# First layer's FFN input projection as seven block products with block sums, and the residual parked in DRAM

## The chip, the cores and the metric

The kernel runs on one core of a Trainium2 chip. The metric is the device time of one execution in microseconds (us). Before the change the median of three runs is 2299.05 us (2296.88 to 2300.37). The engines are named as the profile names them: PE (TensorE matmul), PEld (its weight loads), DVE (VectorE), ACT (ScalarE), POOL (GpSimd), SP (SyncE, which here issues every DMA).

## What is computed

A trunk of two layers over 512 latent tokens and 256 context tokens, 1024 channels. Each layer has a token-mixing block and a SwiGLU FFN with 2816 hidden channels. Only the FFN matters here:

```python
def swiglu(h, w_in, w_out):
    gate, up = jnp.split(h @ w_in, 2, axis=-1)
    return (jax.nn.silu(gate) * up) @ w_out

x = x + g2 * swiglu(modulate(rmsnorm(x, norm2_g[l]), sh2, sc2), w_ffn_in[l], w_ffn_out[l])
```

In the first layer it runs over all 768 tokens, in the second over the 512 latent ones. All data are float32.

## The kernel before

Activations lie with channels on the partitions and tokens along the free axis. A product of float32 data is made as three fp32r matmuls: each operand is split into a rounded part (`hh`, `whi`, written by a cast on ACT) and the rest (`hl`, `wlo`, a subtraction on DVE), and `group_steps` (L193) adds `whi·hh`, `whi·hl` and `wlo·hh` up in one PSUM bank for each of the 128-channel blocks k of the contraction.

The first layer's FFN follows the output projection `wo` (`load_o`, `mul_o`, `done_o`, L1313 to L1327), whose `done_o` leaves the residual in the eight tiles `XT[f]`. `norm_seg` (L285) makes from them the eight tiles each of `hh` and `hl`, the FFN's input (768 tokens wide). Then the 22 hidden tiles of 128 channels are gone through in three chunks, `HID_CHUNKS` (L32). For a hidden tile i, `gate_f` (L1368) and `up_f` (L1376) each load a 128x1024 weight tile, split it, and multiply 8 blocks by 3 matmuls over 512 and over 256 tokens; ACT makes the silu of the gate, DVE multiplies by the up part, ACT and DVE split the result into `hidh` and `hidl`. At a chunk's end the output projection `fo` (`load_f`, `mul_f`, `done_f`, L1387 to L1407) multiplies the chunk's hidden tiles by their rows of `w_ffn_out`, for each of eight output blocks f, and `done_f` adds gate times product to `XT[f]` on DVE. The last chunk goes through `skewed_out` (L342): the latents of the last `SKEW` blocks first, then their context columns, under which the second layer's first norm is made.

Beside this DVE works off a list `bg` of background steps: `mods_rest` (L211) makes the modulation vectors as dot products, one 128x1024 multiply-and-accumulate (L225) for each piece. `bg_step` (L544) puts n of them behind a given DVE instruction; in the FFN it is called after each hidden tile and in each `load_f`, with the rest of the list shared out by `slots`. Where `tc.manual_schedule(engines={PE})` holds, PE's order is that of the program text; elsewhere, and on the other engines, a scheduler lists instructions by program order as they come ready. Every engine then runs its list in order, and so does SP with the DMAs.

SBUF is shared out in tags: 31 `unit` tiles of 128x768 (`hh`, `hl`, `XT`, temporaries), 6 `wide` ones, 3 `whi` and 3 `wlo` of 128x1024, 2 raw weight tiles, 14 `hid` tiles. PSUM has 8 banks: `mm` 3, `s` 2, `t` 2, `o` 1.

## Time and profile before

| | |
|---|---|
| median of 3 runs | 2299.05 us |
| the profiled execution | 2298.55 us, its span 2296.8 us |
| PE busy | 2251.3 us, 98% of the span |
| DVE, ACT, POOL busy | 1447.4, 853.4, 291.0 us |
| mean granted clock of TensorE | 0.993 of full speed |
| DMA | 281 MB, mean 122 GB/s |

A matmul's record in the trace covers its way through the array and overlaps with the next one, so what a matmul costs is read from the distance between starts, not from its duration. The first layer's FFN lies at about 800 to 1355 us: chunk 1 up to 936, its output projection to 1004, then two chunks of seven tiles with theirs.

### The profile page before, as it was taken

To read this page: it belongs to the slowest core of one execution; us is meant where nothing else is said; L and a number is where in the kernel's file an instruction comes from. 1 tells how busy PE (TensorE), PEld (TensorE's weight loads), DVE (VectorE), ACT (ScalarE), POOL (GpSimd) and SP (SyncE) were. 2 spreads that over 40 slices of the span, in tenths; PEclk is the share of its full clock that TensorE was granted. 3 is DMA by queue.
4 is the path that set the end of the run, shared out by engine and by line. 5 is a ranking of instruction groups with operands and counts; after the bars stand their busy time and mean duration, and the time that the engine had idled before them with its cause. 6 is when DMAs were issued, how large, how long until landed. Compare 5 with 4: busy or idle time off the path is not lost.

```text
span 2296.8 us, 33406 instructions
## 1 busy us (share of the span) xinstructions
PE 2251.3 (98%) x12896; PEld 1954.3 (85%) x12896; DVE 1447.4 (63%) x2629; ACT 853.4 (37%) x1612; POOL 291.0 (13%) x294
## 2 busy tenths in 40 slices
PE   8999999999999999999999999999999999999998
PEld 4989899999878888888888888888888778888887
DVE  6887878887776455735522358878877655433334
ACT  5335444445512242112112244555445424222223
POOL 0112211112133010000000021311111221000000
PEclk9999999999999999999999999999999999999999
DMA  7432324444454324524521224233444443423322
GB/s 288 135 101 74 106 95 125 138 125 138 136 201 168 94 92 136 156 89 151 187 70 65 71 95 129 87 118 109 123 124 123 169 165 100 150 93 97 97 95 80
DMA packets 100287, 281.07 MB, mean 122 GB/s; under 512 B 12048, under 2 KB 21408, under 8 KB 100128
## 3 DMA queue, kind: packets, MB, share of 16 engines
q1 hardware_dynamic: 100128, 278.93, 38.0%
q8 instruction: 102, 1.67, 0.3%
q14 instruction: 57, 0.47, 0.1%
HBM read 228.15 MB, written 24.52 MB: 110 GB/s over the span
## 4 chain that ended last, share of the span: by engine, by line
PE 66%; DVE 2%; issue 1%; ACT 1%; DMA 0%; POOL 0%; POOLq 0%; SPq 0%; DVEq 0%; ACTq 0%
PE fg L199 13%; PE fu L199 13%; PE fo L199 13%; PE gt L199 6%; PE wo L199 5%; PE br L199 4%; PE gq L605 2%; PE o L1082 2%; PE s L1005 2%; PE nv L199 1%; PE nk L199 1%; PE pt L1057 1%; PE nq L199 1%; PE ga L199 1%; PE va L199 1%
## 5 line engine op out<-in xcount | busy, mean ns | idle before, releaser
L181 ACT CAST whi<-wraw 128x1024 fp32r<-128x1024 f32 (+1 forms) x274 | 285.2, 1041 | 624.3 <-PE fo L199 181.7
L182 DVE TENSOR_TENSOR wlo<-wraw,whi 128x1024 fp32r<-128x1024 f32 (+1 forms) x274 | 338.6, 1236 | 211.1 <-ACT whi L181 206.2
L1039 POOL TENSOR_SCALAR pt<-pt,sm 128x768 f32<-128x768 f32 (+1 forms) x160 | 147.0, 919 | 760.6 <-DVE sm L1038 513.8
L787 DVE SCALAR_TENSOR_TENSOR y<-u,vec,y 128x783 f32<-128x783 f32 (+1 forms) x240 | 218.4, 910 | 1.5
L199 PE MATMUL gt<-hh,whi 128*128 128x512 f32 (+1 forms) x576 | 212.8, 369 | 0.0
L199 PE MATMUL gt<-hh,wlo 128*128 128x512 f32 (+1 forms) x576 | 205.4, 357 | 0.0
L199 PE MATMUL gt<-hl,whi 128*128 128x512 f32 (+1 forms) x576 | 205.2, 356 | 0.0
L199 PE MATMUL fo<-hidh,whi 128*128 128x512 f32 (+1 forms) x549 | 192.3, 350 | 0.0
L199 PE MATMUL fo<-hidh,wlo 128*128 128x512 f32 (+1 forms) x549 | 191.7, 349 | 0.0
L199 PE MATMUL fg<-hl,whi 128*128 128x512 f32 (+1 forms) x544 | 190.5, 350 | 1.1 <-POOL hl L305 0.8
L199 PE MATMUL fo<-hidl,whi 128*128 128x512 f32 (+1 forms) x549 | 191.5, 349 | 0.0
L199 PE MATMUL fg<-hh,whi 128*128 128x512 f32 (+1 forms) x544 | 190.4, 350 | 1.1 <-ACT hh L300 1.1
L199 PE MATMUL fg<-hh,wlo 128*128 128x512 f32 (+1 forms) x544 | 189.8, 349 | 0.0
L199 PE MATMUL fu<-hh,whi 128*128 128x512 f32 (+1 forms) x536 | 188.5, 352 | 0.6 <-ACT whi L181 0.6
L199 PE MATMUL fu<-hh,wlo 128*128 128x512 f32 (+1 forms) x536 | 188.3, 352 | 0.8 <-DVE wlo L182 0.8
L199 PE MATMUL fu<-hl,whi 128*128 128x512 f32 (+1 forms) x536 | 188.4, 352 | 0.0
L1059 ACT CAST pTh<-pt 128x384 fp32r<-128x384 f32 (+2 forms) x224 | 104.8, 497 | 138.4 <-PE pt L1057 137.6
L1060 DVE TENSOR_TENSOR pTl<-pt,pTh 128x384 fp32r<-128x384 f32 (+2 forms) x224 | 124.0, 569 | 20.2 <-ACT pTh L1059 19.1
L1400 DVE SCALAR_TENSOR_TENSOR xn<-fo,mods,xn 128x512 f32<-128x512 f32 (+1 forms) x75 | 48.3, 644 | 132.7 <-PE fo L199 132.7
L1383 DVE TENSOR_TENSOR sg<-fu,sg 128x512 f32<-128x512 f32 (+1 forms) x67 | 39.9, 596 | 138.3 <-PE fu L199 138.3
L199 PEld LDWEIGHTS gt<-hh,wlo 128*128 128x128 f32 x576 | 109.2, 190 | 16.2
L199 PEld LDWEIGHTS gt<-hh,whi 128*128 128x128 f32 x576 | 109.4, 190 | 11.1 <-ACT gtan L980 0.3
(269 smaller groups left out, 5419.0 us busy)
## 6 DMA issues: line engine op xcount, KB each, us to landing
wraw<-w_in SPq DMA_DIRECT2D x88, 512.0 KB, 3.5
wraw<-w_fi SPq DMA_DIRECT2D x88, 512.0 KB, 3.3
mraw<-wmod_t SPq DMA_DIRECT2D x80, 512.0 KB, 4.2
wraw<-w_fo SPq DMA_DIRECT2D x32, 448.0 KB, 3.3
gd<-gtan SPq DMA_DIRECT2D x48, 256.0 KB, 2.0
wraw<-w_br SPq DMA_DIRECT2D x24, 512.0 KB, 3.4
tg<-gd SPq DMA_DIRECT2D x24, 384.0 KB, 5.1
sraw<-wmod_s SPq DMA_DIRECT2D x16, 512.0 KB, 8.9
```

The lines of the kernel that those rows point to most:

```text
L181: act.copy(hi[:, :n], raw[:, :n])
L182: last_lo[0] = dve.tensor_sub(lo[:, :n], raw[:, :n], f32(hi[:, :n])).ins
L199: pe.matmul(ps[:, :c1 - c0], w[:, k, :], a[k][:, c0:c1], start=i == 0, stop=i == 3 * n - 1)
L605: pe.matmul(ps[:, :256], a[k][:, t * P:(t + 1) * P], w[:, o:o + 256], start=i == 0, stop=i == 3 * KT - 1)
L787: dve.scalar_tensor_tensor(y[:, :YW], u[:, t:t + YW], w, y[:, :YW], ALU.mult, ALU.add)
L1005: pe.matmul(o, Q[:, qc], k, start=i == 0, stop=i == 1)
L1039: pool.tensor_scalar(pt[:, :w], pt[:, :w], sm[:, 3:4], 1.0, ALU.mult, ALU.mult)
L1059: act.copy(hv[:, qi, k0:k0 + step, :], pv)
L1060: dve.tensor_tensor(lw[:, qi, k0:k0 + step, :], pv, f32(hv[:, qi, k0:k0 + step, :]), ALU.subtract)
L1082: pe.matmul(ops[:, o:o + n], v.rearrange("p z d -> p (z d)"), m, start=i == 0, stop=i == len(seq) - 1)
L1383: dve.tensor_mul(sg[:, c0:c1], ps[:, :c1 - c0], sg[:, c0:c1])
L1400: dve.scalar_tensor_tensor(XT[f][:, c0:c1], mrg["pf", f, c0][:, :c1 - c0], mods[l][:, 40 + f, v:v + 1], XT[f][:, c0:c1], ALU.mult, ALU.add)
```

## The change

It touches the first layer's FFN (and a little of what is just ahead of it); the second layer's keeps its form.

- From hidden tile 3 on, gate and up of a tile are made together as a 2x2 block product: the block rows are gate and up (A1., A2.), the block columns of A the first and second four of the eight k blocks, and B is the input cut at the same k and at token 384. Seven block products replace eight (Winograd's form of Strassen's scheme), each of 4 blocks by 3 matmuls over 384 tokens. Sums of weight blocks S1 to S4 are made on POOL, sums of input blocks T1 to T4 once ahead on DVE (`sums_of`, 16 background steps), and split into two fp32r parts each. Weight operands of 128x512 are split one by one (`parts`), two to a `whi`/`wlo` tile. Bank `a` collects A11·B11, S2·T2, S3·T3 and A22·T4 in turn, with copies (`snap`, ACT) of the sums between; bank `b` S1·T1 and S4·B22; bank `c` A12·B21. PE's order is written out by hand: `sw_mid(i)`, `sw_head(i+1)`, `sw_tail(i)`, `sw_head2(i+1)`.
- The chunks of the first layer become six: 3, 4, 4, 4, 3 and 4 hidden tiles (tag `hid` has 2 tiles there instead of 14, the others come from `wide`); the output projection thus runs six times over the eight blocks f, with fewer k each.
- The residual no longer stays in SBUF: `done_o` stores it to `xm` in DRAM, `load_f` reads it back for each f of each chunk, and after `done_f` it is stored again (but for the last chunk).
- The last two blocks of layer 0's modulation (18 background steps) move from the FFN into the `wo` stage, three in each `load_o`.
- The last chunk's `skewed_out` takes a skew of 6 instead of 3.

The core of the diff:

```diff
-HID_CHUNKS = ((0, 8), (8, 7), (15, 7))
+HID_CHUNKS = (((0, 3), (3, 4), (7, 4), (11, 4), (15, 3), (18, 4)), ((0, 8), (8, 7), (15, 7)))
+HALF = 384
@@ ahead of and in the wo stage
             bg_all()
+            if l == 0:
+                for blk in (10, 11):
+                    bg += mods_rest(0, blk)
             def load_o(f):
-                return load_wk(w_out[l, f], KT)
+                wk = load_wk(w_out[l, f], KT)
+                bg_step(3)
+                return wk
@@ done_o
                 square_acc(XT[f], AC, f, c0, c1)
+                if not last:
+                    dma.dma_start(xm[f, :, c0:c1], XT[f][:, c0:c1])
@@ FFN
-            slots = [6 if last else 3 * (NHID - 7) + 8 * 2]
+            chunks = HID_CHUNKS[l]
+            slots = [6 if last else (NHID - 3) + 8 * 5]
+            def sums_of(k):
+                def whole(i):
+                    q[i] = unit("tw")
+                    dve.tensor_add(q[i], f32(hh[k + i]), f32(hl[k + i]))
+                def t12():
+                    t = q["t"] = unit("ts")
+                    a, b = q[0], q[4]
+                    dve.tensor_sub(t[:, 0:HALF], a[:, HALF:TOK], a[:, 0:HALF])
+                    dve.tensor_sub(t[:, HALF:TOK], b[:, HALF:TOK], t[:, 0:HALF])
+                ...
+                def part(n):
+                    ...
+                    act.copy(h, t)
+                    dve.tensor_sub(lo, t, f32(h))
+                return [lambda: whole(0), lambda: whole(4), t12_part, t34_part]
+            def parts(src):
+                if cur[1] % 2 == 0:
+                    cur[0] = [mp.tile([P, 1024], F32R, tag=t, bufs=3, name=t) for t in ("whi", "wlo")]
+                ...
+                act.copy(hi, src)
+                last_lo[0] = dve.tensor_sub(lo, src, f32(hi)).ins
+            def sw_load(i):
+                g, u = [fp_.tile([P, 1024], F32, tag="sr", bufs=2, name="sraw") for _ in range(2)]
+                dma.dma_start(g, w_fi[l, i, 0])
+                dma.dma_start(u, w_fi[l, i, 1])
+            def sw_sum(d, name, a, b, op):
+                t = d[name] = fp_.tile([P, 512], F32, tag="S", bufs=4, name="ssum")
+                pool.tensor_tensor(t, d[a], d[b], op)
+            def sw_mul(d, bank, w, b, first):
+                ...
+                for k in range(4):
+                    for x, y in ((wh, bh), (wh, bl), (wl, bh)):
+                        pe.matmul(d[bank][:, :HALF], x[:, k, :], y[k], start=first and n == 0, stop=n == 11,
+                                  skip_group_check=True)
+            def sw_head(i):
+                sw_load(i)
+                sw_sum(d, "S1", "A21", "A22", ALU.add)
+                sw_sum(d, "S2", "S1", "A11", ALU.subtract)
+                sw_sum(d, "S3", "A11", "A21", ALU.subtract)
+                sw_mul(d, "a", "A11", "B11", True)
+                snap(d, "s1")
+            def sw_head2(i):
+                sw_mul(d, "b", "S1", "T1", True)
+            def sw_mid(i):
+                sw_mul(d, "a", "S2", "T2", False)
+                snap(d, "u2")
+                sw_sum(d, "S4", "A12", "S2", ALU.subtract)
+                sw_mul(d, "c", "A12", "B21", True)
+                dve.tensor_add(sg[:, 0:HALF], d["c"][:, :HALF], d["s1"])
+                act.activation(sg[:, 0:HALF], sg[:, 0:HALF], AF.Silu)
+                sw_mul(d, "a", "S3", "T3", False)
+                snap(d, "u3")
+                dve.tensor_add(d["u3"], d["b"][:, :HALF], d["u3"])
+            def sw_tail(i):
+                sw_mul(d, "a", "A22", "T4", False)
+                dve.tensor_mul(sg[:, 0:HALF], d["a"][:, :HALF], sg[:, 0:HALF])
+                sw_mul(d, "b", "S4", "B22", False)
+                dve.tensor_add(sg[:, HALF:TOK], d["b"][:, :HALF], d["u2"])
+                act.activation(sg[:, HALF:TOK], sg[:, HALF:TOK], AF.Silu)
+                dve.tensor_mul(sg[:, HALF:TOK], sg[:, HALF:TOK], d["u3"])
+                act.copy(q["h"], sg)
+                q["done"] = dve.tensor_sub(q["lo"], sg, f32(q["h"])).ins
             def load_f(f):
-                wk = load_wk(w_fo[l, f, :, k0:k0 + nk, :], nk)
+                if not last:
+                    XT[f] = unit("xt")
+                    dma.dma_start(XT[f], xm[f])
+                src = w_fo[l, f, :, k0:k0 + nk, :]
+                wk = load_wk(src, nk) if last or not lastc else parts(raw_w(src, nk * P)[:, :nk * P])
@@ chunk loop
+                    if not last:
+                        bg[:0] = [x for k in range(4) for x in sums_of(k)]
+                if ci and not last:
+                    while len(T) < 8:
+                        bg_step(1)
+                    manual = tc.manual_schedule(engines={PE})
+                    manual.__enter__()
+                    if ci == 1:
+                        sw_head(k0)
+                        sw_head2(k0)
+                    for i in range(k0, k0 + nk):
+                        sw_mid(i)
+                        if i + 1 < NHID:
+                            sw_head(i + 1)
+                        sw_tail(i)
+                        if i + 1 < NHID:
+                            sw_head2(i + 1)
+                        bg_step(-(-len(bg) // max(1, slots[0])), hid[i]["done"])
+                        slots[0] -= 1
+                    manual.__exit__(None, None, None)
...
-                        bg_step(-(-3 * len(bg) // max(1, slots[0])), hid[i]["done"])
-                    slots[0] -= 3
+                        bg_step(4 if not last else -(-3 * len(bg) // max(1, slots[0])), hid[i]["done"])
...
                             drain(mul_f(f, wk, (c0, c1, v)))
                             done_f(f, (c0, c1, v))
+                        if not last:
+                            dma.dma_start(xm[f], XT[f])
...
-                skewed_out(segs, TQ, load_f, mul_f, done_f, norms, SEG0_AT[2 * l + 1], SEG0_EVERY[2 * l + 1])
+                skewed_out(segs, TQ, load_f, mul_f, done_f, norms, SEG0_AT[2 * l + 1], SEG0_EVERY[2 * l + 1],
+                           SKEW if last else 6)
```

## Rows read from the trace of the kernel before

**Rows 1.** The page's first part: busy us, share of the span, instructions.
```profile
PE 2251.3 (98%) x12896; PEld 1954.3 (85%) x12896; DVE 1447.4 (63%) x2629; ACT 853.4 (37%) x1612; POOL 291.0 (13%) x294
```

**Rows 2.** Windows: stretch, length, busy us (instructions) of PE, PEld, DVE, ACT, POOL; PEclk, DMA share, GB/s.
```profile
836.70:853.40 16.70, 16.70 (x99) 14.78 (x98) 11.24 (x18) 4.54 (x7) 0.00 (x0) 1.00 0.47 158
936.00:1003.00 67.00, 67.00 (x384) 58.58 (x383) 41.83 (x66) 8.74 (x9) 0.00 (x0) 1.00 0.45 142
729.20:799.50 70.30, 69.42 (x395) 60.24 (x394) 30.15 (x42) 18.52 (x27) 3.93 (x4) 1.00 0.32 100
```

**Rows 3.** Waits of PE, 799 to 1360 us, longest entry: us in total, times, longest.
```profile
PE fg L199 <- POOL hl L305: 0.8, 1, 0.8
```

**Rows 4.** Timeline of PE, hidden tiles 1 to 3: start us, duration us, instruction.
```profile
834.16 0.28 PE L199 MATMUL fu<-hh,whi 128*128 128x256 f32 x1
834.28 0.28 PE L199 MATMUL fu<-hl,whi 128*128 128x256 f32 x1
...
836.68 0.40 PE L199 MATMUL fg<-hh,whi 128*128 128x512 f32 x1
...
853.36 0.40 PE L199 MATMUL fg<-hh,whi 128*128 128x512 f32 x1
```

**Rows 5.** Timeline of DVE, first output projection: the drains of two blocks f.
```profile
992.93 0.75 DVE L1400 SCALAR_TENSOR_TENSOR xn<-fo,mods,xn 128x512 f32<-128x512 f32 x1 [3.38 <-PE fo L199]
...
1001.33 0.75 DVE L1400 SCALAR_TENSOR_TENSOR xn<-fo,mods,xn 128x512 f32<-128x512 f32 x1 [3.38 <-PE fo L199]
```

**Rows 6.** Groups by shape, 700 to 1300 us: busy us, mean ns | idle before.
```profile
L225 DVE SCALAR_TENSOR_TENSOR mraw<-mraw,cb 128x1024 f32<-128x1024 f32 x50 | 60.7, 1223 | 22.6 <-DMA mraw<-wmod_t 22.1
...
L1383 DVE TENSOR_TENSOR sg<-fu,sg 128x512 f32<-128x512 f32 x22 | 15.2, 692 | 60.9 <-PE fu L199 60.8
L1384 ACT CAST hidh<-sg 128x512 fp32r<-128x512 f32 x22 | 13.7, 621 | 101.6 <-DVE sg L1383 101.6
...
L1400 DVE SCALAR_TENSOR_TENSOR xn<-fo,mods,xn 128x512 f32<-128x512 f32 x16 | 12.0, 750 | 22.1 <-PE fo L199 22.1
...
L1383 DVE TENSOR_TENSOR sg<-fu,sg 128x256 f32<-128x256 f32 x22 | 9.3, 424 | 16.0 <-PE fu L199 16.0
...
L305 POOL TENSOR_TENSOR hl<-nt,hh 128x512 fp32r<-128x512 f32 x6 | 7.8, 1314 | 9.1 <-ACT hh L304 9.1
...
L1400 DVE SCALAR_TENSOR_TENSOR xn<-fo,mods,xn 128x256 f32<-128x256 f32 x16 | 7.7, 483 | 19.9 <-PE fo L199 19.9
...
L1301 DVE SCALAR_TENSOR_TENSOR yl<-ys,yh 128x768 fp32r<-128x768 f32 x3 | 2.9, 954 | 4.0 <-ACT yh L1300 4.0
```

**Rows 7.** Timeline of POOL and DVE side by side, 639 and 674 us (branch projection).
```profile
639.00 2.00 POOL L590 TENSOR_TENSOR ys<-ys,tg 128x512 f32<-128x512 f32 x2 [17.53 <-DVE tg L589]
639.64 0.42 DVE L589 SCALAR_TENSOR_TENSOR tg<-tg,br 128x256 f32<-128x256 f32 x1 [0.72 <-PE br L199]
...
674.54 2.97 POOL L590 TENSOR_TENSOR ys<-ys,tg 128x512 f32<-128x512 f32 x2 [2.60 <-issue]
674.65 2.26 DVE L225 SCALAR_TENSOR_TENSOR mraw<-mraw,cb 128x1024 f32<-128x1024 f32 x1
676.85 0.08 DVE L225 DVE_READ_ACCUMULATOR mraw<-mraw,cb 128x1 f32 x1
```

**Rows 8.** Timeline of DVE: the end of hidden tile 1.
```profile
839.69 0.42 DVE L1385 TENSOR_TENSOR hidl<-sg,hidh 128x256 fp32r<-128x256 f32 x1
```

**Rows 9.** The page's DMA issues: line, engine, count, KB each, us to landing.
```profile
wraw<-w_fi SPq DMA_DIRECT2D x88, 512.0 KB, 3.3
```

**Rows 10.** Windows of a DMA peak, and of PE idling and its clock (columns of rows 2).
```profile
654.00:656.00 2.00, 1.38 (x8) 0.88 (x7) 2.00 (x5) 0.00 (x0) 0.00 (x0) 1.00 1.01 391
658.00:660.00 2.00, 2.00 (x11) 1.67 (x10) 2.00 (x5) 0.26 (x1) 1.22 (x1) 1.00 1.04 414
...
1361.00:1362.00 1.00, 0.35 (x2) 0.14 (x2) 1.00 (x2) 0.40 (x1) 1.00 (x1) 1.00 0.86 291
1363.00:1366.00 3.00, 3.00 (x14) 2.72 (x14) 1.57 (x3) 1.53 (x3) 1.32 (x2) 0.50 0.28 112
```

More of the change, by code (lines that the diff above doesn't have):

```diff
@@ L162, in trunk @@
     xd = dp.tile([KT, P, TOK], F32, name="xd")
+    xm = dp.tile([KT, P, TOK], F32, name="xm")
     gd = [dp.tile([24, P, TOK], F32, name="gd%d" % l) for l in range(DEPTH)]
@@ L340, in begin, with skewed_out @@
         pump(1)
-    def skewed_out(segs, T, load, mul, done, norms, at, every):
+    def skewed_out(segs, T, load, mul, done, norms, at, every, skew=SKEW):
         s0, s1 = segs
         whole = segs if s0[2] != s1[2] else [(0, T, 0)]
-        n0 = KT - SKEW
+        n0 = KT - skew
         wks = {}
@@ L1362, in hidden @@
                     hid[i] = dict(sg=fp_.tile([P, TOK], F32, tag="sg", bufs=2, name="sg"),
[L1363 to L1365 removed]
+                                  h=fp_.tile([P, TOK], F32R, tag="hid", bufs=HB, name="hidh") if last or i % 4 == 0
+                                  else wide("hidh", F32R)[:, :TOK],
+                                  lo=fp_.tile([P, TOK], F32R, tag="hid", bufs=HB, name="hidl")
+                                  if i % (2 if last else 4) == 0 else wide("hidl", F32R)[:, :TOK])
                 return hid[i]
+            HB = 14 if last else 2
             def gate_f(i, c0, c1, tag=None):
@@ new lines, in sw_mul @@
+            def sw_mul(d, bank, w, b, first):
+                if first:
+                    d[bank] = psum(dict(a="mm", b="s", c="t")[bank], "sw")
+                wh, wl = parts(d[w])
+                bh, bl = side(b)
+                n = 0
+                for k in range(4):
+                    for x, y in ((wh, bh), (wh, bl), (wl, bh)):
+                        pe.matmul(d[bank][:, :HALF], x[:, k, :], y[k], start=first and n == 0, stop=n == 11,
+                                  skip_group_check=True)
+                        n += 1
@@ L1394, in mul_f, with psum_out @@
                 c0, c1, _ = seg
-                ps = mrg["pf", f, c0] = psum_any("fo")
+                ps = mrg["pf", f, c0] = psum_any("fo") if last or lastc else psum_out()
                 yield from group_steps(ps, wk, gh, gl, c0, c1)
+            def psum_out():
+                turn[0] += 1
+                return psum(("mm", "t", "s", "mm", "t")[turn[0] % 5], "fo")
             def done_f(f, seg):
@@ L1422, in trunk @@
                         drain(up_f(1, c0, c1))
-                for i in range(k0, k0 + nk):
+                    if not last:
[18 more added lines that the diff above has]
+                    manual.__exit__(None, None, None)
+                for i in () if ci and not last else range(k0, k0 + nk):
                     if i >= 2:
```

61 lines of the change are left out of this document (54 added, 7 removed).

## The prediction

> **What bounds the kernel now.** I read the engines' busy shares first: PE is busy 98% of the span [rows 1]. Then the windows by stage: in a hidden tile of the first layer's FFN and in its output projection PE is busy for the whole stretch, DVE for 11.24 of 16.70 us at most, ACT for 4.54, POOL not at all [rows 2]. Then PE's waits: over the whole FFN the longest entry is 0.8 us in total [rows 3]. So this stage is a dense row of matmuls, and what a matmul less saves is its distance to the next start. The same rows show what may not grow: DVE has the least room.
>
> **PE, what is removed.** Tile 2 begins at 836.68, tile 3 at 853.36 [rows 4]: 16.68 us for 48 matmuls over 512 tokens and 48 over 256, so one pair costs 0.3475 us; the 256 ones are 0.12 apart [rows 4]. A matmul over 384 tokens is not in the trace; it lies halfway between the two, so I take half a pair, 0.1738 us. A new tile has 7 x 4 x 3 = 84 of them: 14.59 us, each block product 2.085 us. That is 2.09 us less for each of 19 tiles: **39.6 us**, just the eighth of the work. The output projections keep their matmuls (22 x 8 x 3 pairs) and only change their order: 8.40 us for a block f with eight k [rows 5], so 1.05 for each k. PE's floor is therefore 2298.55 - 39.6 = 2259 us; all else can only add to that, but for the handover at the end.
>
> **DVE, POOL and ACT in a new tile.** Prices from rows 6: two inputs of 128x512 on DVE 0.69 us (row of 512), 384 wide (0.692 + 0.424) / 2 = 0.56, 768 wide 0.954; back-to-back instructions start some 0.07 sooner than the sum says (674.65 + 2.26 = 676.91, the next at 676.85) [rows 7]. A tile needs seven splits of 512 (4.85), four additions or products of 384 out of PSUM (2.23), one of 384 within SBUF (0.56) and a split of 768 (0.95): 8.59, less 13 x 0.07, is 7.7 us; a background piece adds 1.25 [rows 6, 7]. POOL has four sums of 512 at 1.31 [rows 6]: 5.3 us. ACT has 12 instructions of at most 512 columns, none over 0.621 by the cast [rows 6], and one of 768, under twice that: below 8.7. Each alone is under 14.6. But POOL and DVE are not independent: the two POOL additions take 2.00 us at 639.00 and 2.97 at 674.54, where a DVE instruction of two SBUF inputs, 1.22 on average, takes 2.26 [rows 6, 7]; the one that reads PSUM at 639.64 keeps its 0.42. If all of it is serial, a tile costs DVE and POOL 7.7 + 5.3 + 1.25 = 14.2 us with one background step and 15.5 with two. The list has 68 steps left behind the sums; by the sharing rule eight go in chunk 0, tiles 3 to 6 get two each, later tiles one.
> The Trainium skill (SBUF — State Buffer, Who interferes with whom) says that a DVE instruction with two SBUF inputs and a POOL instruction that reads SBUF exclude each other for their whole length, and that DVE reading one input from SBUF is free of it; by that rule the four PSUM readers may lie beside POOL, and an estimate is 12.3 and 13.5 us, under PE's time in every tile.
> So the steady state should be PE's, with little to spare. For waits in order at this load I take 0.9 us in tiles 3 to 6 (15.5 - 14.6) and 0.2 in the other 15: **+6.6** (bounds 0 and 1 us a tile, 19). Within a tile the covers are: a copy of bank `a` behind one product (2.085 against a cast of 0.62 and hops), its third behind A11·B11; the single pair of raw tiles is reloaded in 3.3 us [rows 9] and needs a sum and a split more, some 7 us, against four to six products (8 to 12 us) that the three `whi` tiles let the splits run ahead. Both hold, the second with a few us to spare.
>
> **Chunk 0, where DVE runs over.** The sums can't start before tile 1 is done, at 840.0 [rows 8]; tiles 0 to 2 and their projection are unchanged in length (25.2 us at three k), so PE would reach the first new product at 853.4 + 25.2 = 878.6, 38.6 us later. DVE has in that time: T sums, per k four of 768 and four of 384, 6.05 less 0.56, times four, 22.0; eight background pieces 10; eight weight splits of 384, 3.9; eight blocks' drains, 0.750 + 0.483 less 0.14, 8.7 [rows 6]; the rest of tile 2, 3.2; two splits for the new tile, 1.3: 49 us, 53 if POOL's first three sums are in its way. That is 10 to 14 over; drains and pieces that may lag past the end are worth 3.6. I take **+9** (bounds 4 and 17, the latter with one clock fall, priced below).
>
> **The rest.** Chunk ends: the last tile's addition, silu, product, cast and split (0.56 + 0.5 + 0.56 + 0.9 + 0.95, 3.5 us and hops) lie behind S1·T1 of the next tile and nine matmuls of the first k blocks (2.085 + 2.1): 0.3 for each of four. In the last chunk there is no next tile, 2.1 against about 4: 1.9. Sum **+3** (0 to 6). Drains: three more passes of eight blocks cost DVE 26 us, under the output projections, where a block of four k gives 4.2 us for 1.1 + 0.6 + one or two pieces of 1.25: hidden. The residual's traffic there is 0.39 MB in and out for each f, with weights and one modulation tile 1.57 MB in 4.2 us, 374 GB/s, below the 414 that a stretch reaches at a DMA share of 1.04 [rows 10]; on SP a store of `xm[f]` waits for `done_f` and holds up the next weights and residuals behind it, but two raw and three split tiles are ahead. I take 0; without that cover, 0.5 us for each of 40 blocks, 20 us. The `wo` stage gets 16 pieces, 20 us, on a DVE that is busy 30.15 of 70.3 [rows 2], and 16 stores: **+1** at the norm behind it (0 to 3). Skew 6 lengthens the context pass under the second layer's norm (7.4 to 8.6 us) and brings DVE three drains more: 0, bounds -3 and +2.
> Sum: 2298.55 - 39.6 + 6.6 + 9 + 3 + 1 = **2278.6** for the profiled execution; the median stands 0.5 above that one, so 2279.
>
> **Rivals.** (1) *Nearly the whole saving.* DVE clears chunk 0 with 4 us over, POOL hides beside PSUM readers, the steady state has no stall: 2298.55 - 39.6 + 4 + 2 = 2265. For it: each engine alone is well below PE. Against: the 49 us above are counted, not argued.
> (2) *DVE with POOL becomes the bound in the new tiles, slower than before.* 15.5 us serial in a tile, plus what DVE idles in order for a PSUM result while splits wait behind, say 1 us: 16.5 instead of 14.6, 19 x 1.9 = 36; with 13 of the other terms 2308. It decides from 39.6 - 13 = 26.6 us on, 1.4 us a tile, a period of 16.0. For it: 674.54 shows both stretched. Against: two steps come in four tiles only, and PSUM readers are free.
> (3) *The clock.* At 1361 PE was busy 0.35 of 1 us, and the clock then stood at 0.50, the 1.2 GHz level, at 1363 to 1366; with 0.62 us idle at 654 to 656 it stayed at 1.00 [rows 10]. One fall of some 6.5 us at half speed loses 3.3. One in each tile would be 19 x 3.3 = 63, so 2341; from eight falls on nothing is gained. The Trainium skill (TensorE: Matmul & The Clock Gate, A second HAM failure mode: psum-queue depth-cycling) tells of just such short idles between groups of matmuls making the clock oscillate; the row at 654 to 656 speaks against it for idles under 1 us.
> (4) *Saving and stalls cancel*: the SP queue costs the 20 us too: 2298.
>
> **How the numbers follow.** Forecast case (2267 to 2293) 0.61, rival 1 0.12, rival 2 0.15, rival 3 0.04, rival 4 0.08. The measurement tells about 0.2% (4.6 us) from no change: faster 0.73, same 0.08, slower 0.19. The range reaches to PE's floor below and to rival 2's decision and a little past it above: 2260 to 2306.
>
> **What would show it.** Starts 0.174 us apart in a new tile, and seven products in 14.6 to 15.5 us: else the first step is wrong. PE waiting for DVE's `wlo` or for `fo` drains between 855 and 890: the chunk-0 step; if PE is dense there, rival 1. A tile period of 16 us and DVE without idle time: rival 2. PEclk under 1.00 in the FFN: rival 3. PE waiting on weights that waited for SP behind `xm`: rival 4. The forecast falls if the new tiles are neither dense nor DVE-bound, a wait I have not named, such as PSUM or the raw tiles.

## The result, and the profile after

The changed kernel takes 2360.34 us (median of 4 runs, 2359.89 to 2361.18), the kernel before 2298.54 beside it (4 runs, 2296.88 to 2300.37): a ratio of 1.0269, 95% interval 1.0251 to 1.0287. The forecast of a gain was wrong, in sign and by 81 us. The profiled execution spans 2358.1 us, that of before 2296.8.

First the page's part 1 of the changed kernel (busy us, share of the span, instructions), against [rows 1]:

```profile
PE 2243.5 (95%) x12668; PEld 1971.3 (84%) x12668; DVE 1611.7 (68%) x2866; ACT 921.8 (39%) x1777; POOL 411.3 (17%) x370
```

PE is busy 8 us less than before and the span is 61 us longer: PE now waits, which it did not [rows 3]. Where, the windows by stage of the changed kernel tell (columns of [rows 2]). The stages are cut at the start of their first matmul: the first chunk's `w_fo`; the new tiles of chunks 1 to 5; the last chunk's `w_fo`; from there to the second broadcast of the second layer's norm.

```profile
856.32:893.74 37.42, 29.27 (x146) 24.23 (x145) 36.16 (x61) 10.58 (x17) 0.00 (x0) 0.86 0.61 212
893.74:966.61 72.87, 66.61 (x363) 65.02 (x361) 53.31 (x70) 28.20 (x53) 27.43 (x16) 0.95 0.34 113
1002.12:1071.32 69.20, 62.72 (x338) 61.44 (x337) 46.49 (x61) 26.60 (x51) 25.25 (x16) 0.95 0.31 105
1104.81:1170.56 65.75, 61.23 (x339) 59.95 (x338) 43.88 (x57) 26.18 (x50) 26.14 (x16) 0.97 0.33 114
1204.04:1257.12 53.08, 47.55 (x255) 46.27 (x254) 33.11 (x44) 19.96 (x38) 18.22 (x12) 0.94 0.33 113
1284.30:1349.45 65.15, 59.16 (x318) 57.85 (x316) 40.87 (x56) 26.05 (x48) 18.17 (x12) 0.95 0.31 102
1349.45:1406.20 56.75, 42.75 (x200) 36.21 (x200) 23.42 (x39) 13.06 (x22) 1.42 (x5) 0.82 0.40 132
1406.20:1428.10 21.90, 11.16 (x66) 10.15 (x65) 10.60 (x16) 10.99 (x18) 10.20 (x8) 0.69 0.24 79
```

Rows 2 to 6 hold 30, 28, 28, 21 and 26 block products, and three matmuls of `w_fo` among the last (0.7 us). At 2.085 us a product that is 277.3 + 0.7 = 278.0 us; the five windows sum to 326.05. So the new tiles lose 48.1 us, more than the whole saving of 39.6. PE's idle time in them is 326.05 less its busy 297.27, 28.8 us; the other 19.3 are matmuls that took longer than their own time, a part of them at a lower clock (granted 0.94 to 0.97 over the windows). The two windows of before that answer to the last two (the last chunk's `w_fo` with seven k, and the way to the broadcast) are these:

```profile
1296.26:1357.99 61.73, 60.89 (x348) 52.78 (x346) 27.38 (x42) 16.08 (x25) 1.01 (x1) 1.00 0.28 92
1357.99:1371.54 13.55, 11.73 (x65) 10.83 (x65) 9.47 (x13) 10.08 (x16) 7.96 (x7) 0.75 0.37 120
```

Before, the last `w_fo` took 61.73 for 58.8 us of matmuls (seven k at 8.40), 2.9 for sums and broadcast of the norm; after, 56.75 for 33.6 + 2.9, so 20.2 lost, and 8.4 more (21.90 against 13.55) on the way to the broadcast. PE's waits in the changed kernel, 856 to 1428 us (total, times, longest), against the single 0.8 of [rows 3]:

```profile
PE sw L1485 <- ACT sn L1495: 28.6, 19, 3.2
PE ss L249 <- DVE acc L285: 15.6, 2, 8.7
PE fo L204 <- DVE xt L1560: 8.2, 3, 4.4
PE fo L204 <- DVE wlo L187: 6.2, 3, 3.8
```

The first is the loss in the tiles: 19 times PE waits for ScalarE's copy of bank `a`. One such wait, from the timeline of the changed kernel (start us, duration us, engine, instruction, idle time before it and what ended it):

```profile
1004.02 1.14 ACT L1462 CAST whi<-sraw 128x512 fp32r<-128x512 f32 x2 [5.34 <-DMA sraw<-w_fi]
...
1005.99 0.33 SPq L1470 DMA_DIRECT2D sraw<-w_fi  x1
...
1009.25 1.28 POOL L1475 TENSOR_TENSOR ssum<-sraw 128x512 f32<-128x512 f32 x1 [48.01 <-DMA sraw<-w_fi]
1009.27 0.33 PE L1485 MATMUL sw<-hh,wlo 128*128 128x384 f32 x1
1009.44 0.33 PE L1485 MATMUL sw<-hh,whi 128*128 128x384 f32 x1
...
1010.57 0.62 ACT L1462 CAST whi<-ssum 128x512 fp32r<-128x512 f32 x1 [2.97 <-POOL ssum L1475]
...
1011.91 0.62 ACT L1462 CAST whi<-ssum 128x512 fp32r<-128x512 f32 x1 [0.72 <-POOL ssum L1475]
1012.43 0.47 ACT L1495 COPY sn<-sw 128x384 f32<-128x384 f32 x1
...
1012.96 0.88 PE L1485 MATMUL sw<-t,whi 128*128 128x384 f32 x2 [2.31 <-ACT sn L1495]
...
1013.64 0.52 PE L1485 MATMUL sw<-t,wlo 128*128 128x384 f32 x1
```

Read from the bottom. At 1010.65 PE came to the sixth product of tile 7, A22's, and stood 2.31 us for the copy at 1012.43. What is copied there was complete at 1008.4, one product earlier, but in ScalarE's list the copy stands behind the casts of S1 and S2 of tile 8, and these waited for POOL (2.97 and 0.72). POOL waited for the up half of tile 8's raw weights, asked for at 1005.99 and there at 1009.25: the one `sraw` tile of that half was held by A22 of tile 7, which DVE had split at 1005.96. And that split was late in turn: in ScalarE's list A22's cast stands behind the cast of A11 of tile 8 (the two of the row at 1004.02), which waited 5.34 us for the gate half of tile 8, asked for at 998.93. So the two halves' reloads run one behind the other.

Not all 19 waits are of this kind. Of the 28.6 us, 10.0 are waits in which the copy stands behind casts that wait for POOL. Some 12.6, in six waits, are those in which the copy stands behind the first silu, which waits for an addition in DVE's list, where pieces and splits lie ahead of it; the longest is one of them. In the rest it stands behind the casts of the finished hidden tile and the next weights.

```profile
924.19 0.52 ACT L1519 ACTIVATE sg<-sg 128x384 f32<-128x384 f32 x1 [5.27 <-DVE sg L1518]
925.65 1.01 PE L1485 MATMUL sw<-t,whi 128*128 128x384 f32 x2 [3.20 <-ACT sn L1495]
```

After the wait at 1010.65 a matmul takes 0.52 us; before it 0.33, with starts 0.17 apart. The windows behind it show the clock, near its lower level (0.50, 1.2 GHz), and that it came back to the upper one (2.4 GHz); the third stands behind a wait of 1.53 us at 1249.19:

```profile
1013.00:1017.00 4.00, 4.00 (x14) 4.00 (x15) 3.48 (x5) 1.32 (x3) 2.25 (x2) 0.57 0.05 14
1017.00:1020.00 3.00, 3.00 (x19) 3.00 (x18) 1.47 (x3) 1.13 (x3) 0.00 (x0) 1.00 0.49 161
1250.72:1254.72 4.00, 4.00 (x23) 4.00 (x24) 3.19 (x4) 0.75 (x2) 2.30 (x2) 1.00 0.36 126
```

In this trace the clock falls seven times in the five windows, each time at one of the seven waits of 2.16 to 3.2 us and at none of the twelve of 1.53 us or less. The length alone does not decide: in the tiles of `e3_no_sums` waits of 2.24, 2.62 and 3.20 us were followed by no fall, two of 2.12 and 3.33 us were.

In the last chunk the place is SP's queue. Its timeline in the changed kernel (L1567 is the store of a finished block to `xd`, L1542 the load of the next residual block):

```profile
1355.59 0.33 SPq L1567 DMA_DIRECT2D xd<-xt  x1
1355.97 0.42 SPq L1542 DMA_DIRECT2D xt<-xm  x1
1361.24 0.32 SPq L1567 DMA_DIRECT2D xd<-xt  x1
1361.61 0.42 SPq L1542 DMA_DIRECT2D xt<-xm  x1
```

Each load stands right behind the store of the block before, which waits for that block's drain; the next drain then waits for the load, PE for the bank. DVE's wait in that stage, 1349 to 1406 us:

```profile
DVE xt L1560 <- DMA xt<-xm: 13.7, 5, 5.3
```

### The profile page after: what moved, and what is told of

Its sections match the earlier page's. It is cut to its first block, busy times and chain, and to the rows that moved or that the text cites. A ratio compares the mean times of both kernels' runs of the same rounds, so it can differ in the third digit from the quotient of the medians.

```text
span 2358.1 us, 33861 instructions
## 1 busy us (share of the span) xinstructions
PE 2243.5 (95%) x12668; PEld 1971.3 (84%) x12668; DVE 1611.7 (68%) x2866; ACT 921.8 (39%) x1777; POOL 411.3 (17%) x370
## 5 line engine op out<-in xcount | busy, mean ns | idle before, releaser
L186 ACT CAST whi<-wraw 128x1024 fp32r<-128x1024 f32 (+3 forms) x252 | 244.3, 969 | 538.8 <-PE fo L204 126.4
L187 DVE TENSOR_TENSOR wlo<-wraw,whi 128x1024 fp32r<-128x1024 f32 (+3 forms) x252 | 292.8, 1162 | 139.9 <-ACT whi L186 134.5
L204 PEld LDWEIGHTS fo<-hidh,whi 128*128 128x128 f32 x549 | 106.4, 194 | 29.6 <-DVE xt L1560 5.2
L1475 POOL TENSOR_TENSOR ssum<-sraw 128x512 f32<-128x512 f32 x38 | 61.9, 1630 | 387.2 <-DMA sraw<-w_fi 280.6
L204 PEld LDWEIGHTS fo<-hidh,wlo 128*128 128x128 f32 x549 | 106.5, 194 | 22.1 <-DVE wlo L187 7.5
L204 PEld LDWEIGHTS fo<-hidl,whi 128*128 128x128 f32 x549 | 106.6, 194 | 15.7 <-DVE hidl L1535 0.8
L204 PEld LDWEIGHTS gt<-hl,whi 128*128 128x128 f32 x576 | 109.2, 190 | 10.8 <-issue 0.2
L1010 PE MATMUL s<-ks,qs 128*128 128x256 f32 (+1 forms) x576 | 112.8, 313 | 5.5 <-ACT pt L1033 2.1
L1485 PE MATMUL sw<-t,whi 128*128 128x384 f32 x304 | 87.9, 373 | 28.6 <-ACT sn L1495 28.6
L230 DVE SCALAR_TENSOR_TENSOR mraw<-mraw,cb 128x1024 f32<-128x1024 f32 x80 | 103.4, 1293 | 11.3 <-DMA mraw<-wmod_t 11.1
```

Source lines behind the costliest of these rows:

```text
L186: act.copy(hi[:, :n], raw[:, :n])
L187: last_lo[0] = dve.tensor_sub(lo[:, :n], raw[:, :n], f32(hi[:, :n])).ins
L204: pe.matmul(ps[:, :c1 - c0], w[:, k, :], a[k][:, c0:c1], start=i == 0, stop=i == 3 * n - 1)
L230: dve.scalar_tensor_tensor(o, raw, 1.0, cb[:, v, :], ALU.mult, ALU.mult, accum_out=st["s"][:, c:c + 1])
L1010: pe.matmul(o, Q[:, qc], k, start=i == 0, stop=i == 1)
L1475: pool.tensor_tensor(t, d[a], d[b], op)
```

## The experiments

All are edits of the changed kernel. Executions of one kernel lie up to 0.3% (6 us) off their median, so where a kernel has one time only, the stage and its waits decide, not the total. The same code can differ by stage too: the first `w_fo` begins anywhere from 853.9 to 861.5 us in runs that are alike up to there, and the new tiles, the same in the changed kernel, `e1_hoist` and `e5_hoist_skew4`, lose 48.1, 45.4 and 49.0 us. Losses in the tiles are counted as above, from start to start, against 278.0 us; the expectations counted to the end of the last matmul, 1 to 1.5 us more.

**One suspect at a time.**

`e1_hoist`: the last chunk's residual loads are issued ahead of its first `w_fo` block.

```diff
                     continue
+                if not last:
+                    for f in range(KT):
+                        XT[f] = unit("xt")
+                        dma.dma_start(XT[f], xm[f])
                 AC = unit("acc")
```

> The changed kernel, but in the first layer's last chunk all eight residual loads are issued ahead of its output projection, so that no load stands behind a store of a finished block in SP's list. Nothing else is touched. Theory Q (in SP's list each load xt(f+1) stands behind the store xd(f), which waits for block f: one block at a time, 5 to 7 us each): the stretch from the end of the last new tile to the second layer's first projection falls from 57 us to 36 or less, and the whole from 2360 to 2330 to 2340. Rival (the drains and the norm's chain on DVE are slow, or the DMAs themselves): less than 6 us.

2345.36 us. The last `w_fo` takes 38.25 instead of 56.75, 1.8 over its matmuls: SP's order was worth 18.5 us, and this is shown, though the stretch stays 2 us over the expected 36. The total misses its range by 5, and as much lies ahead of the edit: the first `w_fo` begins at 861.50 instead of 856.32. The way to the broadcast stayed long:

```profile
1352.05:1390.30 38.25, 35.35 (x200) 30.06 (x200) 23.68 (x39) 13.30 (x22) 2.22 (x5) 1.00 0.54 185
1390.30:1413.49 23.19, 11.61 (x67) 10.69 (x65) 11.38 (x16) 10.88 (x18) 9.73 (x8) 0.71 0.23 75
```

`e2_copies_first`: the casts of the next tile's S1 and S2, and the first silu, are put behind the third copy in ScalarE's list.

```diff
-                sw_mul(d, "b", "S1", "T1", True)
+                behind_u3(d, "b", "S1", "T1", True)
...
-                sw_mul(d, "a", "S2", "T2", False)
+                behind_u3(d, "a", "S2", "T2", False)
```

> The changed kernel with ACT's list altered in one way: the splits of the next tile's S1 and S2 and the first silu are put behind the third copy of bank a. Theory A (the copy waits in ACT's list behind splits of sums that POOL has not made yet): PE's waits for the copies fall from 28.6 us to under 8 and the 49 us that the 19 new tiles cost beyond 14.6 us each fall to 20 to 30; the whole 2330 to 2345. Theory B (DVE and POOL keep each other from working, DVE is late whatever ACT's order): the 49 us stay within 8.

2352.37 us; the tiles lose 33.2 instead of 48.1. PE's wait for the copies, 890 to 1350 us, falls from 28.6 to this:

```profile
PE sw L1491 <- ACT sn L1501: 16.7, 9, 3.1
```

All three numbers miss what theory A said (under 8, 20 to 30, 2330 to 2345). The list's order is part of it, not the root: ahead of the copy, in five of the nine waits that stay, ScalarE's cast of raw weights had itself waited for the load, by 1.2 to 4.5 us.

`e3_no_sums`: POOL makes no sums, the products take plain blocks.

```diff
                 t = d[name] = fp_.tile([P, 512], F32, tag="S", bufs=4, name="ssum")
-                pool.tensor_tensor(t, d[a], d[b], op)
...
-                wh, wl = parts(d[w])
+                wh, wl = parts(d[dict(S1="A21", S2="A11", S3="A11", S4="A12").get(w, w)])
```

> The changed kernel without the weight sums S1 to S4: POOL does none, and the products take plain weight blocks in their place (this leaves out part of the computation). Loads, splits, products, copies and drains stay. Theories A and B both: the 49 us beyond 14.6 a tile fall below 10, the whole 2315 to 2325. If more than 25 us stay, the loss is neither the sums' lateness nor POOL against DVE, but the reload of the raw tiles or the order of the lists.

2331.43 us; the tiles still lose 24.4. With no work on POOL at all PE waits for splits, 890 to 1340 us:

```profile
PE sw L1484 <- ACT whi L1462: 15.0, 7, 3.3
```

In all seven waits ScalarE's cast had just waited for the load of the raw weights. So a loss of this kind needs no sum: the reload of the raw tiles alone makes one. How much of the 48.1 it is doesn't follow, since the blocks put in the sums' place read the gate half one product longer (A12 for S4) and so make its reload later than it is in the changed kernel.

`e4_two_raw_pairs`: a second pair of raw tiles, by taking the gate half from the raw tiles that `w_fo` uses.

```diff
-                g, u = [fp_.tile([P, 1024], F32, tag="sr", bufs=2, name="sraw") for _ in range(2)]
+                g = mp.tile([P, 1024], F32, tag="wraw", bufs=2, name="sraw")
+                u = fp_.tile([P, 1024], F32, tag="sr", bufs=2, name="sraw")
```

> The changed kernel with two raw tiles each for the gate and for the up weights instead of one (the gate's from the tag that the output projections use). Theory A: the next tile's loads no longer wait for this tile's splits, POOL's sums come 5 us or more sooner, the 49 us fall below 20, the whole 2325 to 2340. Theory B: POOL works the same and holds DVE the same, the 49 us stay within 8.

2331.80 us. Windows of the tiles of chunks 2 and 3 (28 products each; two matmuls of chunk 2 lie ahead of its window):

```profile
1006.17:1064.41 58.24, 58.24 (x337) 58.24 (x336) 43.77 (x61) 26.93 (x50) 22.78 (x16) 1.00 0.35 117
1097.89:1156.49 58.60, 58.60 (x339) 58.60 (x338) 42.02 (x59) 26.85 (x51) 22.43 (x16) 1.00 0.40 133
```

PE has no idle time, none of the 19 waits for copies is left in any chunk, and four tiles take what 28 products cost by the prediction (58.4), while POOL makes all its sums (22.8 us) and DVE all its splits. Over all five chunks some 6 us are lost, 5 of them in the first. That settles the tiles: the reload, with all that waits for it, and not POOL or DVE. The price is in `w_fo`, whose loads share the raw tiles now (below).

**The next suspects.** `e5_hoist_skew4`: as `e1_hoist`, and four instead of six blocks left over for the context in the last chunk.

```diff
-SEG0_AT = ((7, 15), (10, 16), (5, 9), (5, 12))
+SEG0_AT = ((7, 15), (10, 15), (5, 9), (5, 12))
...
-                           SKEW if last else 6)
+                           SKEW if last else 4)
```

> The run with the eight residual loads ahead (2345.4 us), and in the last chunk four instead of six of w_fo's blocks left over for the context, with the latents' broadcast asked for after 15 instead of 16 steps. Theory: with six left over, the square of the last context block stands in ScalarE's list behind all eight of the latents' normed blocks, so TensorE waits 10.1 us for the context's column sums; with four it stands behind two, the wait falls under 2 us, the stretch from the last matmul of w_fo to the second broadcast from 23.2 to 13 to 15 us, and the kernel to 2334 to 2338 us. Rival: with fewer context matmuls behind the latents' sums TensorE runs dry at the broadcast instead, the wait only moves, and the kernel stays at 2343 to 2347 us.

2336.76 us, as expected; the way from the last `w_fo` matmul to the broadcast takes 13.15 us, where before has 13.55 and `e1_hoist` 23.19 (in later runs with the same edit up to 15.9). What had held it shows in ScalarE's timeline of `e1_hoist`: the square of the last context block behind the latents' normed blocks.

```profile
1403.50 0.62 ACT L309 CAST hh<-nt 128x512 fp32r<-128x512 f32 x1
1404.03 0.41 ACT L284 ACTIVATE sq<-xt 128x256 f32<-128x256 f32 x1
```

With four left over that square runs at 1393.89, behind two of the eight.

`e6_raw_chunk0`: as `e4_two_raw_pairs`, without the modulation pieces beside the first chunk's `w_fo`.

```diff
-                bg_step(-(-len(bg) // max(1, slots[0])))
+                if last or ci > 0:
+                    bg_step(-(-len(bg) // max(1, slots[0])))
+                elif f < 4:
+                    bg_step(2)
```

> The run with two pairs of raw tiles (2331.8 us), and no modulation piece in the first chunk's w_fo stage (they come later, beside the new tiles); the sums stay. Theory: that stage took 41.0 us there with 10.5 us of idle TensorE because VectorE had sums, drains and eight pieces of 1.22 us to do; without the eight it takes 29 to 32 us and the kernel 2321 to 2324 us. Rival: it is the order (sums ahead of drains in VectorE's list), not the amount: it stays over 37 us and the kernel over 2328. If the pieces only move the loss into the tiles, the stage is shorter and the kernel the same.

2327.25 us: between the two expectations. The stage takes 32.65 us, just over the 29 to 32 of the theory, against 41.12 with the pieces, so the amount of DVE's work did matter; but the third chunk's `w_fo`, 33.5 us there, takes 41.3 here and gives most of it back. Why it does is not shown.

`e7_sums_unused`: the sums are made and not used (the second edit of `e3_no_sums` alone).

> Leaves out part of the computation: GpSimd makes the four sums of each tile as in the changed kernel, but the products take plain blocks in their place, so nobody waits for a sum. Theory of lateness (the raw tiles' reload and what waits for the sums): some 26 to 35 us lost in the new tiles, like the run without any sums (25.9), and the kernel 2332 to 2342 us. Theory that GpSimd's work slows VectorE: the loss stays near the changed kernel's 49 us, and the kernel at 2352 us or more.

2350.89 us; the tiles lose 31.2, within the range for lateness (26 to 35). The total lies nearer the other theory's, but by other stages: the first `w_fo` begins 3.0 us later than in the changed kernel and the third takes 4.2 longer. Against `e3_no_sums`, with the same products, POOL's work costs 6.8 us; the change from here to the changed kernel, where the products wait for the sums, 16.9. Lateness is the larger part. The 6.8 us are not far above the 3.6 by which the same tiles differ between runs, and they need late loads to be felt: `e4_two_raw_pairs` has the slower DVE too and loses nothing by it.

`e8_combined`: `e4`, `e5` and `e6` together.

> The four edits together: two pairs of raw tiles, the eight residual loads ahead of the last chunk, four blocks left over for the context, no modulation piece in the first chunk's w_fo stage. If each is worth what it is worth alone (28.5, 15, 9 and 9 us) the kernel falls from 2360.3 to about 2299 us, within 2293 to 2305, so no faster than the kernel before (2293.9 beside the first four runs, 2298.5 in the timed ones) beyond what can be measured. If the gains overlap or the moved pieces come back as stalls in the tiles, over 2308 us.

2302.18 us (10 runs), ratio 1.0022 (1.0012 to 1.0031), as expected. The tiles are dense from the first to the last, and yet the kernel is no faster than before. What is left lies in `w_fo`: the second chunk's takes 40.37 us, and ScalarE waits there and in the tiles for `w_fo`'s weights (886 to 1310 us):

```profile
ACT whi L186 <- DMA wraw<-w_fo: 105.1, 23, 12.6
```

**The same memory, cut finer.** `e9_quarters`: four raw tiles of 128x512 instead of two of 128x1024, A12 and A22 changing places in every second new tile, so that no load waits for the late A22 of the tile before but that of A12, which is needed last.

```diff
-                g, u = [fp_.tile([P, 1024], F32, tag="sr", bufs=2, name="sraw") for _ in range(2)]
-                dma.dma_start(g, w_fi[l, i, 0])
-                dma.dma_start(u, w_fi[l, i, 1])
+                for a in ("A11", "A21", "A22", "A12") if i % 2 else ("A11", "A21", "A12", "A22"):
+                    d[a] = fp_.tile([P, 512], F32, tag="sr", bufs=4, name="sraw")
+                for a in ("A11", "A21", "A22", "A12"):
+                    o = 512 * (a[2] == "2")
+                    dma.dma_start(d[a], w_fi[l, i, int(a[1]) - 1, :, o:o + 512])
```

> The changed kernel with the same memory for raw tiles, cut into four tiles of 128x512 in place of two of 128x1024, so that each is free once its own readers are done; every second new tile takes A12's and A22's places in exchange, so that A22, whose cast comes last and which the next tile's first sum needs, is loaded where A12 was. Theory: what stops the new tiles is not the amount of raw memory but that A22's late cast holds the next tile's load; then the new tiles lose under 8 us of their 49, as with two pairs of raw tiles, and w_fo's stages, which shared the raw tiles there, are as short as in the changed kernel; the kernel at 2315 to 2325 us. Rival: the load has to be a whole tile ahead; then copies still wait for GpSimd's sums, some 20 us stay, and the kernel is at 2332 us or more.

2327.52 us, 2.5 over the range; the tiles lose 11.2 instead of 48.1, somewhat more than the "under 8": 6.3 of idle PE and 4.9 of longer matmuls. Two of the five windows, and PE's wait for the copies:

```profile
894.85:960.63 65.78, 63.90 (x363) 62.46 (x362) 50.62 (x70) 27.30 (x53) 24.30 (x16) 1.00 0.39 129
998.47:1059.58 61.11, 59.42 (x338) 58.37 (x337) 45.53 (x60) 25.76 (x49) 23.80 (x16) 1.00 0.31 104
```

```profile
PE sw L1486 <- ACT sn L1496: 6.1, 9, 1.2
```

The same bytes in the same memory are enough for most of it. The waits that stay are 0.7 us each on average, and the clock stays at 1.00 in all five windows.

`e10_combined_quarters`: `e8_combined` with the quarters in place of the shared pair.

> The four edits of the combined run, with quarter raw tiles in place of the second pair that shared w_fo's raw tiles. Theory: the combined run's w_fo stages of the second, third and fifth chunk take 40.4, 41.0 and about 31 us where 33.6, 33.6 and 25.2 us of matmuls stand, because their casts wait for w_fo loads whose buffers the new tiles' loads hold; without the sharing some 14 us come back and the kernel takes 2284 to 2291 us. If it is VectorE's drains instead, 2297 to 2303 us as before.

2289.35 us, as expected; the second, third and fifth `w_fo`, 40.4, 41.0 and about 31 us in `e8_combined`, take 34.5, 35.5 and 26.7: the sharing was the cause.

`e11_quarters_sums_early`: that, with the sums eight instead of four at a time behind the first chunk's tiles.

```diff
-                        bg_step(4 if not last else -(-3 * len(bg) // max(1, slots[0])), hid[i]["done"])
+                        bg_step(8 if not last else -(-3 * len(bg) // max(1, slots[0])), hid[i]["done"])
...
-                elif f < 4:
+                elif f < 0:
```

> The run before this one, and the sums of the normed blocks made eight instead of four at a time behind the first chunk's second and third tile, none beside its w_fo stage. Theory: that stage (32.8 us in the combined run, 25.2 us of matmuls) is held by VectorE's sums standing ahead of its drains; 3 to 6 us come back, and the kernel takes 2280 to 2287 us, 0.5 to 0.8% faster than the kernel before. Rival: the sums delay the third tile's own drains and splits by as much, and the kernel is where the run before this one is, within 2 us.

2301.75 us (11 runs), ratio 1.0021 (1.0012 to 1.0030): slower than `e10_combined_quarters`, which neither theory said. The first chunk's `w_fo`, here and in `e10_combined_quarters`:

```profile
855.65:894.76 39.11, 28.53 (x147) 24.48 (x145) 26.67 (x45) 8.80 (x15) 0.00 (x0) 0.87 0.56 194
```

```profile
856.93:886.75 29.82, 27.73 (x148) 23.43 (x147) 28.34 (x48) 10.73 (x17) 0.00 (x0) 0.94 0.58 205
```

DVE has less to do in it (26.67 against 28.34) and it is 9.3 us longer. DVE's list holds two whole rounds of sums ahead of the first drain, which comes at 872.48; PE stands 5.93 us for it, and a `w_fo` load then lands so late that ScalarE waits for it:

```profile
889.45 0.51 ACT L186 CAST whi<-wraw 128x384 fp32r<-128x384 f32 x1 [13.55 <-DMA wraw<-w_fo]
```

So in that stage it is the order, once the amount fits.

`e12_quarters_timed`: the kernel of `e10_combined_quarters`, timed.

> The combined run with quarter raw tiles again, timed: the one look gave 2289.35 us, some 0.35% under the kernel before beside it (2297.06). Theory: its stages (tiles 65.9, 60.9, 60.6 and 45.5 us for 30, 28, 28 and 21 products, w_fo 29.8, 34.6, 35.7, 33.7, 26.9) show 20 to 25 us of the 39.6 us of matmuls that the blocks save still lost in seven places, so it is faster by 0.2 to 0.5%. If the look was a lucky one, it is within 0.2%.

2291.62 us (6 runs), the kernel before 2297.92 beside it (10 runs): ratio 0.9968 (0.9956 to 0.9980), within the expected 0.2 to 0.5%.

`e13_quarters_copies_first`: that, with the edit of `e2_copies_first`.

> That kernel with the next tile's casts of the first two sums, and the silu, put behind the third copy out of bank a in ScalarE's list, as in the run with the copies first. Still open: whether what is left in the new tiles (6.5 us of waits for copies, and 3.3, 2.5, 2.2 and 1.5 us over the matmuls' own 62.6, 58.4, 58.4 and 43.8) is the list's order alone. Theory: with the load in time the copies stand behind nothing but those casts, so the waits fall under 2 us and the kernel gains 4 to 8 us more, to 2282 to 2286. Rival: the casts put later make the following products wait for their splits instead, and the kernel gains nothing or loses up to 5 us.

2288.32 us (5 runs, 2283.28 to 2291.67), ratio 0.9957 (0.9944 to 0.9970): 0.43% faster than the kernel before, but over the expected 2282 to 2286. The intervals of the two runs overlap, so that the copies' order is worth its expected 4 to 8 us is not shown by the times; the tiles lose 6.6 instead of the 10.5 to 11.2 of the four runs with quarters and without it, and PE's waits for the copies fall to 3.3 us, not under 2. Windows of `e13_quarters_copies_first`: the first `w_fo`, the tiles of chunks 1 to 5, the last `w_fo`, the way to the broadcast.

```profile
857.26:887.34 30.08, 27.82 (x147) 23.38 (x146) 28.32 (x48) 10.69 (x17) 0.00 (x0) 0.94 0.59 205
```

```profile
887.34:951.79 64.45, 63.09 (x361) 62.45 (x360) 48.45 (x68) 27.39 (x53) 24.45 (x16) 1.00 0.41 140
986.21:1045.76 59.55, 59.03 (x338) 58.45 (x337) 45.77 (x64) 25.70 (x50) 23.77 (x16) 1.00 0.39 132
1080.54:1140.28 59.74, 59.12 (x338) 58.48 (x337) 42.37 (x58) 25.58 (x50) 23.16 (x16) 1.00 0.40 138
1173.77:1218.07 44.30, 44.20 (x255) 43.88 (x253) 31.40 (x42) 19.00 (x37) 18.35 (x12) 1.00 0.41 139
1244.40:1300.99 56.59, 55.70 (x317) 54.81 (x316) 38.54 (x56) 25.29 (x48) 17.67 (x12) 1.00 0.35 116
1300.99:1340.31 39.32, 35.52 (x201) 30.01 (x200) 24.77 (x43) 14.01 (x25) 2.14 (x5) 1.00 0.54 194
1340.31:1356.22 15.91, 12.50 (x64) 11.59 (x65) 8.30 (x12) 10.20 (x16) 9.67 (x8) 0.68 0.23 75
```

## Why the prediction was wrong, step by step

The sum again, with what each term came to. Each entry is a stage's time over its matmuls' own (or over the same stretch of before), from the windows and from the starts of the stages in PE's timeline.

| term (us) | predicted | changed kernel | `e13` |
|---|---|---|---|
| matmuls saved | -39.6 | -39.6 | -39.6 |
| start of the first chunk's `w_fo` (pieces beside `wo`) | +1 | +2.9 | +3.9 |
| first chunk's `w_fo` | +9 | +12.2 | +4.9 |
| new tiles | +6.6 | +48.1 | +6.6 |
| `w_fo` of chunks 1 to 4, chunk ends | +3 | +3.7 | +3.0 |
| last chunk's `w_fo` | 0 | +20.2 | +2.8 |
| way to the second broadcast | 0 | +8.4 | +2.4 |
| from there to the end | 0 | +4.7 | +5.0 |
| sum | -20.0 | +60.6 | -11.0 |
| measured, span against 2296.8 | | +61.3 | -10.3 |

**The saving was right.** A matmul over 384 tokens costs what half a pair [rows 4] was said to cost: 28 products in `e4_two_raw_pairs` take 58.60 us with PE busy throughout, 2.09 each against 2.085. The 39.6 us are there in every version; the question was what is put on top.

**The step that failed** is the sentence on covers in a new tile, above all "the single pair of raw tiles is reloaded in 3.3 us [rows 9] and needs a sum and a split more, some 7 us, against four to six products (8 to 12 us) that the three `whi` tiles let the splits run ahead. Both hold". The length of the chain that it counts was right: in the wait shown above it takes 6.9 us from the load's start at 1005.99 to the end of the copy at 1012.90, 3.26 of it the load. But the pair was taken as one reload, and there are two, one behind the other: the up half's could not start before A22's cast, which stands behind A11's, which waited for the gate half. And the cover was counted to the wrong end. 8 to 12 us is the time to the product that uses the sum: S1's would have come at 1014.8, 8.8 us after 1005.99, and its split was in time. But ScalarE works its list in order, and behind the casts of S1 and S2 stands the copy that PE needs two products earlier, at 1010.65. For that there were 4.7 us. The other cover, "a copy of bank `a` behind one product (2.085 against a cast of 0.62 and hops)", failed at the same place: I counted the copy's length and not what stands ahead of it, which in 12.6 of the 28.6 us is a silu that waits for DVE's list and not the sums' casts. The bounds of this term (0 and 19) came from DVE and POOL as throughput; the loss was latency. The prediction named the raw tiles last, among the things that would make it fall, and gave them no chance.

**The clock made it dearer.** Of the 48.1 us, 28.8 are PE's idle time and 19.3 longer matmuls. Not all of these are the clock's: by the windows' granted clocks the seven falls cost some 15 us at most, and `e9_quarters` has 4.9 us of longer matmuls with the clock at 1.00 throughout. Rival 3 priced one fall in each of 19 tiles at 3.3 us; seven came, at some 2 us each. The clock alone did not decide: the 28.8 us of waits are by themselves over the 26.6 that rival 2 gave as the limit. The Trainium skill (TensorE: Matmul & The Clock Gate, A second HAM failure mode: psum-queue depth-cycling) says that frequent short idles between groups of matmuls cost throughput by letting the clock oscillate; the trace agrees, with 0.57 at 1013 to 1017 and 1.00 from 1017 to 1020. I had set the row at 654 to 656 [rows 10] against that rule, where 0.62 us of idle changed nothing. That row holds for what it shows: in `e9_quarters`, with nine waits of at most 1.2 us, the windows stay at 1.00. My error was to use it as if the idles would stay that short.

**DVE and POOL** were not the bound (rival 2 falls), though DVE's list stands behind six of the changed kernel's 19 waits: with all sums made, DVE is busy 43.77 of 58.24 us in `e4_two_raw_pairs`. The term of 6.6 us is what `e13` loses, but that is luck: it was set for the changed kernel and for DVE's and POOL's load, and `e13` loses it by waits for copies, 3.5 us of idle PE and 3.1 of longer matmuls.

**The start of the first chunk's `w_fo`** (+2.9 against +1) is a sum of unlike parts: `wo` takes 1.6 us more (71.96 against 70.38), the first tiles 4.1 more (57.82 against 53.74, with a wait of PE for DVE of 2.34 us at the norm), and `wo` begins 2.7 us earlier, in code that the change leaves alone. With starts from 853.9 to 861.5 in the runs it says little.

**The first chunk's `w_fo`** was right in kind and size: +12.2 against +9, within 4 and 17, and PE waited where the text said it would, for `wlo` and for drains; one more clock fall lies in it (0.86). That it was the amount of DVE's work alone was too simple; `e11_quarters_sums_early` shows the order to be worth 9 us.

**SP's queue** got 0, with 20 us as the price without cover, and in the last chunk the price fell due: 20.2. The store that waits for a drain was named, and the cover, "two raw and three split tiles are ahead", is one for weights. The residual block has none: its load stands behind the store of the block before, and the drain that needs it comes 4 us later. In chunks 1 to 4, where the store goes to `xm`, the cover held (3.7 us for the four). I looked at who queues behind the store and stopped at the weights.

**Skew 6** got 0 with bounds of -3 and +2; it cost 8.4. I counted more context work for PE and three drains more for DVE. What costs is where the context's squares land in ScalarE's list, and `e5_hoist_skew4` gives it all back (13.15 against 13.55); `e13`, with the same skew, keeps 2.4 of it, at a granted clock of 0.68.

**Rival 4**, saving and stalls cancel by SP's queue, had the right mechanism in the last chunk only. **Rival 1** is excluded by the first chunk alone.

**Left open.** From the second broadcast to the end every version takes 930 to 931.6 us where before takes 925.3 (930.0 in the changed kernel, 930.3 in `e13`). The traces say where: up to the second layer's branch projection, 415.9 us behind the broadcast, PE's starts agree to 0.1 us; its FFN begins 1.6 us later, that FFN's first `w_fo` 3.5, the end 4.7. PE's idle time there is 16.1 us against 13.1, one wait of 1.8 us (for DVE's `ys`) among it that before lacks. Why is not shown.

## What to carry to other kernels

When work is cut into smaller products, write down for every single-buffered tile which instruction is its last reader, and follow the reload from there through every in-order list that it enters: the first instruction on the critical engine that needs anything behind it in such a list sets the time that it has, not the product that uses the data. Freeing a buffer in parts, by reader, can do most of what a second buffer does: the same 8 KB a partition in four pieces took the tiles' loss from 48.1 to 11.2 us, a second pair to some 6. And where an engine works its list in order, price a cheap instruction by what stands ahead of it (a copy of 0.47 us cost PE 2.31; a load on SP 18.5 us in eight blocks), and count how long the single waits are: in the tiles of these runs most of those over 2.1 us were paid a second time in clock, and none under 2 us.

## What the runs showed of the hardware

DVE's splits (two SBUF inputs, 128x512) are longer where POOL makes sums: groups by shape, 1002 to 1170 us of the changed kernel and 993 to 1152 us of `e3_no_sums`, where POOL has no work (count, busy us, mean ns):

```profile
L1463 DVE TENSOR_TENSOR wlo<-ssum,whi 128x512 fp32r<-128x512 f32 x30 | 33.6, 1124 | 13.5 <-ACT whi L1462 12.7
```

```profile
L1463 DVE TENSOR_TENSOR wlo<-sraw,whi 128x512 fp32r<-128x512 f32 x53 | 35.2, 689 | 19.5 <-ACT whi L1462 19.4
```

1.124 us against 0.689 (0.98 with the changed kernel's 23 splits of raw weights), while DVE's 384-wide additions out of PSUM stay at 0.55 to 0.56 in both. That is the exclusion of the Trainium skill (SBUF — State Buffer, Who interferes with whom), which the prediction cited; the traces agree with both halves of it. What had not been expected is how little it matters here: some 6.8 us when the loads are late, nothing that can be seen when they are in time.

The versions that beat the kernel before scatter more than it does, and with the clock: the five runs of `e13` go from 2283.28 us at a mean granted clock of 0.994 to 2291.67 at 0.991, the kernel before from 2294.82 to 2298.96.
